# A hybrid Mamba-2 and block-attention trunk: x and the parameters handed over by channel, the weights in tiles

## Chip, cores and metric

The kernel runs on one core of a Trainium2 chip. The metric is the device time of one execution in microseconds (us). Most executions of one kernel agree within 0.3%.

## What is computed

Batch 1, 256 positions, 2048 channels, float32. One Mamba-2 layer, then keys and values from its output, one attention layer, and a last norm (all attention is within one block of 256 positions, so the reference's choice of blocks picks nothing):

```python
def reference(x, ...):
    h = rmsnorm(x, a_norm_g)                 # (1, 256, 2048)
    proj = h @ a_w_in                        # 2048 x 10304: z 4096, xBC 6144, dt 64
    xbc = silu(causal_depthwise_conv(proj[xBC], conv_w, conv_b))    # 4 taps: x 4096, B 1024, C 1024
    dt = softplus(proj[dt] + dt_bias); a = dt * -exp(A_log)
    y = ssd_chunked_scan(x * dt, a, B, C) + D * x                   # one chunk of 256
    y = grouped_rmsnorm(y * silu(z), gnorm_g, 8)
    x = x + y @ a_w_out                      # 4096 x 2048
    k, v = split(rmsnorm(x, kv_norm_g) @ w_kv); k = rope(k)         # 2048 x 4096
    q, z = split(rmsnorm(x, b_norm_g) @ b_w_in); q = rope(q)        # 2048 x 4096
    x = x + (causal_softmax_attention(q, k, v) * silu(z)) @ b_w_out # 16 heads of 128; 2048 x 2048
    return rmsnorm(x, final_norm_g)
```

## The kernel before

**The products.** Every large product is cut into blocks of 512 output columns, and a block into units of two k (a k is 128 channels of the contraction), so a unit has 256 x 512 weights, 512 KB. A unit goes through four steps: SP's queue loads it (`load`, tile `raw`, 4 buffers); ScalarE rounds it to the fast matmul format (`hi<-raw`); VectorE takes the rest (`lo<-raw,hi`; `hi` and `lo` have 5 buffers); TensorE multiplies it (`products`). The left operand is split in the same way into two halves (`hT` for the first layer, later `yn`, `kvop`, `bop`, `oop`), and a product of two split numbers is three matmuls of 128x512 each: high by high, low by high, high by low. There are two halves j of 128 positions, so a unit is 12 matmuls, and the sums `ps` of a block fill two banks of PSUM. Four banks are kept for such sums, the other four ("s") for transposes and small products.

**The order.** The program is written out in one order per engine. The list `ORDER` names the blocks of the first layer: `B0 d0 C0 x0 z0 ...` (B, C, x, z are columns of `a_w_in`; `d0` is the narrow dt block of 16 matmuls, one per k; `o` and `p` multiply by `a_w_out`). The main loop runs over the units `u`; it first emits the splits of units up to a look-ahead, each followed by the load of the unit four further on, and then the products of `u`. Between products, `some` emits pieces of side work (convolution, scan, norms, attention) when a model of the engines' clocks in the program says that their inputs are ready. So what is emitted early moves where later side work stands.

**The start.** `xl` holds x by position (two tiles of 128 positions, 2048 channels), loaded in four parts by `load_x`. For each of the 16 k, `h_gen` transposes both parts of x on TensorE (`s<-ident,xl`), and `operand` scales by the gain `g_a` and splits into `hT` (ScalarE the high half, VectorE the low). Three such k precede the first product, the other 13 stand between the products of block B0, whose units are u = 0 to 7. The gain itself comes as 16 rows (`ga`) and is transposed too. `squares` sums x squared along the channels, per position, in ScalarE and VectorE (`accum_out`). `first_norm` turns that into the factor `r` (`root`: a Sqrt on ScalarE and small VectorE steps). `parameters` transposes the other vectors on TensorE (`s<-ident,em`), which GpSimd's queue had loaded into `em`.

**After a block.** `turn` scales the finished bank by `r` (ScalarE `ps<-ps,r`), transposes 32x32 blocks on VectorE (`T<-ps`), writes to DRAM on SP's queue (`turned<-T`) and reads it back with GpSimd's queue (`U<-turned`, four transfers), which leaves the block by channel in `U`. `dt_evac` has TensorE transpose `r` right behind the dt block (`s<-ident,r`).

Of the kernel before, what the change touches and what calls it, by code (L numbers as in the profile page):

```python
# [173 lines left out]
def trunk_kernel(ctx: ExitStack, tc: tile.TileContext, x, a_norm_g, a_w_in, a_conv_w, a_conv_b,  # L174
                 a_dt_bias, a_A_log, a_D, a_gnorm_g, a_w_out, kv_norm_g, w_kv, b_norm_g, b_w_in,
# [134 lines left out]
    def load(u):  # L310
        if u >= len(units) or units[u][2] == 1:
            return
        b, k, _ = units[u]
        if b["form"] == "dt":
            t = wts.tile([P, 16, 64], F32, name="raw_dt", tag="raw")
            src = dram(b["w"], b["col"], [[b["ncols"], P], [P * b["ncols"], 16], [1, 64]])
# [37 lines left out]
    accs = {}  # L354
# [6 lines left out]
    def products(u):  # L361
        b, k, row = units[u]
        acc = accs.setdefault(id(b), {})
        if b["form"] == "dt":
            ps, w = bank("ps_dt"), HI.pop(u)
            for i in range(16):
                PE.matmul(ps, lhsT=w[:, i, :], rhs=b["operand"](i), start=i == 0, stop=i == 15)
            b["evac"](ps)
            some(4)
            return  # L370
        hi, lo, k0, k1 = HI.pop(u), LO.pop(u), b["ks"][0], b["ks"][-1]
        last = k + 1 == k1
        rows = (0, 1) if row is None else (row,)
        for j in rows:
            if k == k0:
                acc[j] = bank("ps")
            for i in range(2):
                xo = b["operand"](k + i)
                first, end = k + i == k0, k + i == k1
                xh, xl = xo[:, j * P:(j + 1) * P], xo[:, L + j * P:L + (j + 1) * P]  # L380
                PE.matmul(acc[j], lhsT=xh, rhs=hi[:, i, :], start=first, stop=False)
                PE.matmul(acc[j], lhsT=xl, rhs=hi[:, i, :], start=False, stop=False)
                PE.matmul(acc[j], lhsT=xh, rhs=lo[:, i, :], start=False, stop=end)
                if not end:
                    some(2)
            if last:
# [41 lines left out]
    ga = const.tile([16, P], F32, name="ga", tag="c1")  # L428
    SP.dma_start(ga, dram(a_norm_g, 0, [[P, 16], [1, P]]))
    xl = [big.tile([P, D], F32, name=f"xl{t}", tag=f"y{4 + t}") for t in range(2)]  # L430
    xv = x[0].rearrange("(t p) d -> p t d", p=P)

    def load_x(h):
        for t in range(2):
            SP.dma_start(xl[t][:, h * 512:(h + 1) * 512], xv[:, t, h * 512:(h + 1) * 512])  # L435

    load_x(0)
# [3 lines left out]
    em = take("em")  # L441
    vec = em[:112, 1, :P]
    row = 0
    for src, n in ((a_conv_b, 48), (a_gnorm_g, 32), (kv_norm_g, 16), (b_norm_g, 16)):
        POOL.dma_start(vec[row:row + n, :], dram(src, 0, [[P, n], [1, P]]))
        row += n
    cwr = em[:, 0, :256].rearrange("p (a b) -> p a b", a=2)[:96]
    POOL.dma_start(cwr, dram(a_conv_w, 0, [[P, 96], [96 * P, 2], [1, P]]))
    dta = const.tile([64, 2], F32, name="dta")
    POOL.dma_start(dta[:, 0:1], dram(a_dt_bias, 0, [[1, 64], [1, 1]]))  # L450
    POOL.dma_start(dta[:, 1:2], dram(a_A_log, 0, [[1, 64], [1, 1]]))
    dr = const.tile([32, 2], F32, name="dr")
    POOL.dma_start(dr, dram(a_D, 0, [[2, 32], [1, 2]]))
# [48 lines left out]
    early = big.tile([P, 2, 1024], F32, name="early", tag="y6")  # L502
# [9 lines left out]
    g_a = const.tile([P, 16], F32, name="g_a")  # L512
    pa = take("s")
    PE.transpose(pa[:, :16], ga, ident[:16, :16])
    ACT.activation(g_a, pa[:, :16], AF.Copy)
    banks.give((pa.tensor.name, pa.offset))
# [16 lines left out]
    gv = const.tile([P, 112], F32, name="gv")  # L533
    cbias = const.tile([P, 48], F32, name="cbias")
    g_gn, g_kv, g_b = gv[:, 48:80], gv[:, 80:96], gv[:, 96:112]
    dw = em[:32, 1, P:2 * P].rearrange("p (a b) -> p a b", a=2)
    Dv = const.tile([P, 32], F32, name="Dv")
    cw = const.tile([P, 192], F32, name="cw")
    negA = const.tile([64, 1], F32, name="negA")

    def parameters():

        p = take("s")
        PE.transpose(p[:, 0:32], dw.rearrange("p a b -> p (a b)"), ident[:32, :32])
        PE.transpose(p[:, 128:224], cwr[:, 0, :], ident[:96, :96])
        PE.transpose(p[:, 224:320], cwr[:, 1, :], ident[:96, :96])
        PE.transpose(p[:, 320:432], vec, ident[:112, :112])
        ACT.activation(Dv, p[:, 0:32], AF.Copy)
        ACT.activation(cw, p[:, 128:320], AF.Copy, scale=0.5)
        ACT.activation(gv, p[:, 320:432], AF.Copy)  # L550
        give(p, em)
        DVE.tensor_scalar(cbias, gv[:, 0:48], 0.5, None, op0=OP.mult)
# [19 lines left out]
    def h_gen():  # L572
        for k in range(16):
            p = take("s")[:, :L]
            for t in range(2):
# [3 lines left out]
            banks.give((p.tensor.name, p.offset))  # L579
# [389 lines left out]
    for name in ORDER:  # L969
        kind, i = name[0], int(name[1:])  # L970
        names[len(blocks)] = name
        if kind == "d":
            block(a_w_in, NIN, DI + CONV, range(16), h_op, "dt", dt_evac, "h")
        elif kind in "BCxz":
            col = {"B": 2 * DI, "C": 2 * DI + 1024, "x": DI, "z": 0}[kind] + 512 * i
            evac = {"B": lambda q: conv_evac(32 + 4 * q, ("B", q)), "C": c_evac, "x": x_evac, "z": z_evac}[kind](i)
            block(a_w_in, NIN, col, range(16), h_op, "x", evac, "h")
        else:
# [4 lines left out]
            block(a_w_out, D, 512 * n, ks, lambda k: yn[k // 4][:, k % 4, :], "x", out_evac(n, i < 10 and kind == "o", kind == "p"), "yn")  # L983
# [162 lines left out]
    for n in range(4):  # L1146
        block(w_kv, 2 * D, 512 * n, range(16), lambda k: B["kvop"][:, k, :], "x", k_evac(n), "kv")
    for n in range(4):
        block(w_kv, 2 * D, D + 512 * n, range(16), lambda k: B["kvop"][:, k, :], "x", v_evac(n), "kv")
    for kind, n in ("z0", "q0", "q1", "q2", "z1", "q3", "z2", "z3"):  # L1150
        n = int(n)
        if kind == "q":
            block(b_w_in, 2 * D, 512 * n, range(16), b_op, "x", q_evac(n), "b")
        else:
            block(b_w_in, 2 * D, D + 512 * n, range(16), b_op, "x", zb_evac(n), "b")
# [59 lines left out]
    for n in range(4):  # L1215
        block(b_w_out, D, 512 * n, range(16), lambda k: B["oop"][:, k, :], "rows" if n == 3 else "x",
# [7 lines left out]
    for h in range(1, 3):  # L1224
        load(2 * h - 2)
        load(2 * h - 1)
        load_x(h)
    part = split(0)
    for i in range(2):
        next(prep)  # L1230
        if not i:
            warm_up()
        part(i)
    next(prep)
    banks.give((warm.tensor.name, warm.offset))
    load(4)
    begun = 1
    for u in range(len(units)):
        while begun <= min(u + (1 if u < 7 else u - 5 if u < 7 + LOOK else LOOK), len(units) - 1):
            split(begun)()  # L1240
            load(begun + RAW_BUFS)
            if begun == 1:
                load_x(3)
            begun += 1
        if u in (1, 3, 5, 6):
            squares(u // 2)
        if u == 7:
            first_norm()
        if u == 2:
            DVE.tensor_copy(dw, dr[:, :, None].to_broadcast([32, 2, 64]))  # L1250
        if u == 7:
            parameters()
        b, k, _ = units[u]
# [12 lines left out]
_INS = ['x', 'a_norm_g', 'a_w_in', 'a_conv_w', 'a_conv_b', 'a_dt_bias', 'a_A_log', 'a_D', 'a_gnorm_g', 'a_w_out',  # L1266
        'kv_norm_g', 'w_kv', 'b_norm_g', 'b_w_in', 'b_w_out', 'final_norm_g']
# [13 lines left out]

# [21 lines left out]
```

## Time and profile before

| what | value |
|---|---|
| timed runs | 1135.43, 1135.71 (median), 1139.35 us |
| span of the profiled execution | 1140.6 us |
| TensorE busy | 1123.2 us (98%), 5153 matmuls |
| VectorE, ScalarE, GpSimd busy | 852.6, 643.9, 145.1 us |
| DMA | 267.29 MB, 234 GB/s mean |
| granted TensorE clock, mean | 0.996 |

The span runs from the first to the last instruction or landing of one execution taken by the profiler; the page gives no other time for that execution. It lies 4.9 us above the median of the timed runs and 1.2 us above the slowest. Line 130 in the rows is the wrapper through which every instruction of TensorE, VectorE and ScalarE is recorded, so rows are told apart by their tiles. In a row of a timeline stand the start and duration in us, the engine, the operation, `output<-inputs`, the shapes and a count; in square brackets the idle time before it and what ended it.

### The profile page before, as it was taken

What the parts mean: (1) busy time and instruction counts of PE and PEld (TensorE: products, weight loads), DVE (VectorE), ACT (ScalarE), POOL (GpSimd) and SP (SyncE); (2) the same over time, 40 slices, a digit from 0 to 9 for tenths busy, and PEclk for the clock granted to TensorE, in tenths of its full rate; (3) what the DMA queues carried; (4) which work ended last, traced back from release to release, by engine and by line L of the source; (5) the groups of instructions that cost most, each with busy time, mean ns of one, the idle gap of its engine ahead of it and who ended that gap; (6) DMA issues with size and microseconds to landing.
All of it is one profiled execution on the core that took longest, in us unless ns stands there. A gap on an engine that the chain in (4) does not pass through costs nothing.

```text
span 1140.6 us, 14865 instructions
## 1 busy us (share of the span) xinstructions
PE 1123.2 (98%) x5153; PEld 918.7 (81%) x5153; DVE 852.6 (75%) x1316; ACT 643.9 (56%) x896; POOL 145.1 (13%) x255
## 2 busy tenths in 40 slices
PE   9999999999999999999999999999999999999996
PEld 6887888888787888888888888878888888888885
DVE  5786968877868969697987667877445687797564
ACT  5566757765857757567654574434443444444453
POOL 2011121121011021112111000000000011222000
PEclk9999999999999999999999999999999999999999
DMA  8778999897887888888887557768757777989752
GB/s 264 221 230 236 272 251 288 243 284 219 243 246 223 255 242 264 253 237 252 263 253 238 194 178 222 203 200 245 238 172 243 214 224 241 269 247 260 254 202 92
DMA packets 133403, 267.29 MB, mean 234 GB/s; under 512 B 13712, under 2 KB 14560, under 8 KB 133200
## 3 DMA queue, kind: packets, MB, share of 16 engines
q1 hardware_dynamic: 120384, 230.20, 64.9%
q0 software_dynamic: 12944, 36.15, 13.4%
q8 instruction: 40, 0.66, 0.2%
q14 instruction: 35, 0.29, 0.1%
HBM read 240.03 MB, written 26.28 MB: 233 GB/s over the span
## 4 chain that ended last, share of the span: by engine, by line
PE 81%; DVE 7%; DMA 6%; issue 3%; ACT 2%; POOL 0%; SPq 0%; DVEq 0%; ACTq 0%; POOLq 0%
PE ps L130 76%; PE s L130 5%; DMA U<-turned 2%; DVE lo L130 2%; DVE xs L130 2%; DMA raw<-in_a_w_in_dram 1%; DVE T L130 1%; DMA raw<-in_w_kv_dram 1%; ACT hi L130 1%; DMA turned<-T 1%; DVE K L130 1%; POOL U L415 0%; ACT xs L130 0%; ACT u L130 0%; SPq L435 0%
## 5 line engine op out<-in xcount | busy, mean ns | idle before, releaser
L130 DVE TENSOR_TENSOR lo<-raw,hi 128x1024 fp32r<-128x1024 f32 (+1 forms) x385 | 463.5, 1215 | 172.6 <-ACT hi L130 171.6
L130 ACT ACTIVATE hi<-raw 128x1024 fp32r<-128x1024 f32 (+1 forms) x385 | 397.3, 1051 | 261.4 <-PE ps L130 120.1
L130 PE MATMUL ps<-hi,hT 128*128 128x512 f32 x1280 | 399.7, 393 | 0.2 <-DVE hT L130 0.2
L130 PEld LDWEIGHTS ps<-hi,hT 128*128 128x128 f32 x1280 | 238.1, 188 | 49.0 <-issue 0.7
L130 PE MATMUL ps<-lo,hT 128*128 128x512 f32 x640 | 250.5, 391 | 0.0
L130 PE MATMUL ps<-hi,bop 128*128 128x512 f32 x512 | 160.7, 395 | 0.0
L130 PE MATMUL ps<-hi,yn 128*128 128x512 f32 x512 | 159.5, 393 | 0.0
L130 PE MATMUL ps<-hi,kvop 128*128 128x512 f32 x512 | 158.4, 390 | 0.0
L415 POOL DMA_DIRECT2D U<-turned x128 | 74.2, 586 | 654.3 <-DMA turned<-T 293.0
L130 PEld LDWEIGHTS ps<-lo,hT 128*128 128x128 f32 x640 | 120.6, 188 | 27.2 <-DVE lo L130 2.0
L130 PEld LDWEIGHTS ps<-hi,bop 128*128 128x128 f32 x512 | 95.8, 188 | 19.5
L130 PEld LDWEIGHTS ps<-hi,kvop 128*128 128x128 f32 x512 | 95.6, 188 | 19.6
L130 PEld LDWEIGHTS ps<-hi,yn 128*128 128x128 f32 x512 | 94.8, 188 | 19.7 <-issue 0.7
L130 PE MATMUL ps<-lo,kvop 128*128 128x512 f32 x256 | 100.0, 390 | 2.2 <-DVE lo L130 2.2
L130 PE MATMUL ps<-lo,yn 128*128 128x512 f32 x256 | 100.1, 391 | 0.7 <-DVE lo L130 0.7
L130 PE MATMUL ps<-lo,bop 128*128 128x512 f32 x256 | 99.7, 389 | 0.0
L130 PE MATMUL ps<-hi,oop 128*128 128x512 f32 x256 | 79.6, 392 | 0.0
L130 DVE SCALAR_TENSOR_TENSOR xs<-u,cw,xs 128x255 f32<-128x255 f32 (+2 forms) x144 | 59.3, 476 | 0.0
L130 PEld LDWEIGHTS ps<-lo,kvop 128*128 128x128 f32 x256 | 48.0, 188 | 13.0 <-DVE lo L130 3.1
L130 PEld LDWEIGHTS ps<-lo,yn 128*128 128x128 f32 x256 | 48.1, 188 | 11.6 <-DVE lo L130 1.5
L130 PEld LDWEIGHTS ps<-lo,bop 128*128 128x128 f32 x256 | 48.1, 188 | 10.3
L130 PEld LDWEIGHTS ps<-hi,oop 128*128 128x128 f32 x256 | 47.9, 188 | 9.8
(172 smaller groups left out, 944.9 us busy)
## 6 DMA issues: line engine op xcount, KB each, us to landing
raw<-in_a_w_in_dram SPq DMA_DIRECT2D x159, 512.0 KB, 5.3
raw<-in_a_w_out_dram SPq DMA_DIRECT2D x64, 512.0 KB, 5.5
raw<-in_w_kv_dram SPq DMA_DIRECT2D x64, 512.0 KB, 4.7
raw<-in_b_w_in_dram SPq DMA_DIRECT2D x64, 512.0 KB, 5.0
turned<-T SPq DMA_DIRECT2D x64, 256.0 KB, 4.6
U<-turned POOLq DMA_DIRECT2D x128, 128.0 KB, 6.8
raw<-in_b_w_out_dram SPq DMA_DIRECT2D x32, 512.0 KB, 5.5
em<-AC POOLq DMA_DIRECT2D x32, 256.0 KB, 7.4
```

What stands on the lines that cost most here:

```text
L130: return call(out, *args, **kw)
L415: POOL.dma_start(U[32 * q:32 * q + 32].rearrange("p (b c) -> p b c", b=8), src)
```

## The change

The host hands over x a second time by channel (`xT`, 128 x 16 x 256), all per-channel vectors as one array of 128 rows (`params`), the two per-head vectors as `heads`, and every weight matrix as tiles of 256 x 512, in which one of the 128 partitions has its two rows side by side (4 KB where it was 2 KB twice).

- x is loaded by channel into `xt` (nine loads, two of 1 k and seven of 2 k); `hT` is made from it with no transpose. The 32 transposes of x, the one of the gain and the four of the parameters are gone.
- The parameters come with two loads on SP's queue behind the split of unit 3; the gain `g_a` comes with a load on ScalarE's own queue. GpSimd's eight loads at the start are gone. The halving of two vectors is moved to VectorE, at u = 9.
- The squares of x are now summed by channel: ScalarE squares 512 columns (2 k), VectorE adds them to a running sum, eight times. The sum over the 128 channels of a partition block is four matmuls by a column of ones (`s<-ones,early`), in the middle of the dt block, behind its sixth matmul.
- The norm's factor therefore comes later: `first_norm` stands in the dt block, and the two results of B0 are held until then (`held`). Before, `first_norm` stood ahead of B0's last unit and the results left at its end.
- The look-ahead at u = 7, 8, 9 is 1, 2, 3 units where it was 2, 3, 4.

```diff
-        if u in (1, 3, 5, 6):
-            squares(u // 2)
+        if 1 <= u <= 7:
+            squares(u - 1)
         if u == 7:
-            first_norm()
-        if u == 2:
-            DVE.tensor_copy(dw, dr[:, :, None].to_broadcast([32, 2, 64]))
-        if u == 7:
+            squares(7)
             parameters()
...
     def squares(h):
-        ACT.activation(early[:, 0, :512], xl[0][:, h * 512:(h + 1) * 512], AF.Square, accum_out=ss[:, 0, h:h + 1])
-        v = xl[1][:, h * 512:(h + 1) * 512]
-        DVE.scalar_tensor_tensor(early[:, 1, :512], v, 1.0, v, op0=OP.mult, op1=OP.mult, accum_out=ss[:, 1, h:h + 1])
+        total, s = early[:, 0, :512], early[:, 1, h % 2 * 512:(h % 2 + 1) * 512]
+        v = xt[h // 4][:, h % 4 * 2:h % 4 * 2 + 2, :].rearrange("p k l -> p (k l)")
+        ACT.activation(s if h else total, v, AF.Square)
+        if h:
+            DVE.tensor_add(total, total, s)
...
     def first_norm():
-        DVE.tensor_reduce(nt[:, 0, :], ss, axis=mybir.AxisListType.X, op=OP.add)
+        p = take("s")
+        for t in range(2):
+            for i in range(2):
+                PE.matmul(p[:, t:t + 1], lhsT=early[:, 0, i * L + t * P:i * L + (t + 1) * P], rhs=ones[:, 0:1],
+                          start=i == 0, stop=i == 1)
+        DVE.tensor_copy(nt[:, 0, :], p[:, 0:2])
         root(nt, D)
...
             for i in range(16):
+                if i == 6:
+                    first_norm()
+                    for acc, j in held:
+                        blocks[0]["evac"](acc, j)
                 PE.matmul(ps, lhsT=w[:, i, :], rhs=b["operand"](i), start=i == 0, stop=i == 15)
...
     def h_gen():
         for k in range(16):
-            p = take("s")[:, :L]
-            for t in range(2):
-                PE.transpose(p[:, t * P:(t + 1) * P], xl[t][:, k * P:(k + 1) * P], ident)
-            operand(hT[:, k, :], p, g_a[:, k:k + 1])
+            operand(hT[:, k, :], xt[k // 8][:, k % 8, :], g_a[:, k:k + 1])
...
-            t = wts.tile([P, 2, 512], F32, name="raw", tag="raw")
-            src = dram(b["w"], k * P * b["ncols"] + b["col"], [[b["ncols"], P], [P * b["ncols"], 2], [1, 512]])
...
+            t = RAW[0] if half else wts.tile([P, 2, 512], F32, name="raw", tag="raw")
+            if half is None:
+                SP.dma_start(t.rearrange("p i c -> p (i c)"), b["w"][b["n"], k // 2])
```

Three places show what moves. First, TensorE's own list from the start of the program: `early` is a tile of ones for warm-up matmuls. Before:

```order
L130 MATMUL s<-ident,xl_76 128x128
L130 MATMUL s<-ident,xl_77 128x128
L130 MATMUL ps<-hi,hT 128x512 x2
L130 MATMUL ps<-lo,hT 128x512
L130 MATMUL ps<-hi,hT 128x512 x2
L130 MATMUL ps<-lo,hT 128x512
```

and at the dt block and what follows it:

```order
L130 MATMUL ps_dt<-hT,dtp 128x512 x16
L130 MATMUL s<-ident,r_113 128x128 x2
L130 MATMUL ps<-hi,hT 128x512 x2
L130 MATMUL ps<-lo,hT 128x512
L130 MATMUL ps<-hi,hT 128x512 x2
```

After, the same place at the dt block:

```order
L130 MATMUL ps_dt<-hT,dtp 128x512 x6
L130 MATMUL s<-ones,early 128x1 x4
L130 MATMUL ps_dt<-hT,dtp 128x512 x10
L130 MATMUL s<-ident,r_99 128x128 x2
L130 MATMUL ps<-hi,hT 128x512 x2
```

The pair of transposes that stood in front of every sixth product of B0 is gone, and four matmuls of one column stand in the dt block.

Second, ScalarE around the first norm, from the split of the dt weights (`dtp`) to the results of B0. Before:

```order
L130 ACTIVATE dtp<-raw_dt 128x16x64
L130 ACTIVATE hi<-raw 128x1024
L130 ACTIVATE r_113<-r_113 128x2
L130 ACTIVATE Dv<-s 128x32
L130 ACTIVATE cw<-s 128x192
L130 ACTIVATE gv<-s 128x112
L130 ACT_TABLE_LOAD
L130 ACTIVATE negA<-dta 64x1
L130 ACTIVATE ps<-ps,r_113 128x512 x2
```

After:

```order
L130 ACTIVATE dtp<-raw_dt 128x16x64
L130 ACTIVATE early<-xt_77 128x512 x2
L130 ACT_TABLE_LOAD
L130 ACTIVATE negA<-dta 64x1
L130 ACTIVATE hi<-raw 128x1024 x2
L130 ACT_TABLE_LOAD
L130 ACTIVATE r_99<-r_99 128x2
L130 ACTIVATE ps<-ps,r_99 128x512 x2
L130 ACTIVATE dtw<-ps_dt 64x256
```

The Exp for `negA` now stands ahead of the Sqrt for `r`, so the Sqrt needs its table again, and a third load follows later for the next Exp; two splits stand ahead of the Sqrt.

Third, VectorE where the second convolution of C ends (`xs<-u,xs`), to which TensorE's product of C with B (`s<-xs`) comes later. Before:

```order
L130 TENSOR_TENSOR lo<-raw,hi 128x1024
L130 SCALAR_TENSOR_TENSOR xs<-u,cw,xs 128x255 x4
L130 SCALAR_TENSOR_TENSOR xs<-u,cw,xs 128x254 x4
L130 TENSOR_TENSOR lo<-raw,hi 128x1024
L130 SCALAR_TENSOR_TENSOR xs<-xs,Dv,s 128x256 x2
L130 SCALAR_TENSOR_TENSOR xs<-u,cw,xs 128x253 x4
L130 TENSOR_TENSOR lo<-raw,hi 128x1024
L130 SCALAR_TENSOR_TENSOR xs<-xs,Dv,s 128x256 x2
L130 TENSOR_TENSOR lo<-raw,hi 128x1024
L130 SCALAR_TENSOR_TENSOR xs<-u,xs 128x1024
```

After:

```order
L130 TENSOR_TENSOR lo<-raw,hi 128x1024
L130 TENSOR_TENSOR xs<-xs,z_1873 128x512
L130 SCALAR_TENSOR_TENSOR xs<-u,par,xs 128x254 x4
L130 TENSOR_TENSOR lo<-raw,hi 128x1024 x2
L130 TENSOR_TENSOR squares<-squares 128x512
L130 TENSOR_TENSOR squares<-squares 128x256
L130 SCALAR_TENSOR_TENSOR xs<-u,par,xs 128x253 x4
L130 TENSOR_TENSOR lo<-raw,hi 128x1024 x2
L130 SCALAR_TENSOR_TENSOR xs<-u,xs 128x1024
```

The convolution's last four steps lie over more `lo`. Counted from the first product, TensorE's first product of this C with B stands behind 1444 main products instead of 1426, and VectorE's step that it needs stands behind one `lo` more. For the first C the numbers are 382 instead of 379, behind as many `lo` as before. Other side work of the first layer moves by up to 108 products either way; from the attention layer on, the orders are the same but for a few neighbours.

More of the change, by code (lines that the diff above doesn't have):

```diff
@@ L282, in trunk_kernel, with block @@
     blocks = []
-    def block(w, ncols, col, ks, operand, form, evac, key):
-        blocks.append(dict(w=w, ncols=ncols, col=col, ks=ks, operand=operand, form=form, evac=evac, key=key))
+    def block(w, n, ks, operand, form, evac, key):
+        blocks.append(dict(w=w, n=n, ks=ks, operand=operand, form=form, evac=evac, key=key))
     units = []
@@ L308, in trunk_kernel, with load @@
     loads, copies, ended = [0.0], [0.0], {}
-    def load(u):
+    def load(u, half=None):
         if u >= len(units) or units[u][2] == 1:
@@ L385, in products @@
                     some(2)
-            if last:
+            if last and u == 7:
+                held.append((acc[j], j))
+            elif last:
                 b["evac"](acc[j], j)
@@ L425, in in_32s, with load_x @@
         return a.rearrange("p j (b l) -> p j b l", l=32)
-    ga = const.tile([16, P], F32, name="ga", tag="c1")
-    SP.dma_start(ga, dram(a_norm_g, 0, [[P, 16], [1, P]]))
-    xl = [big.tile([P, D], F32, name=f"xl{t}", tag=f"y{4 + t}") for t in range(2)]
+    g_a = const.tile([P, 16], F32, name="g_a")
+    nc.scalar.dma_start(g_a, params[:, :16])
+    xt = [big.tile([P, 8, L], F32, name=f"xt{t}", tag=f"y{4 + t}") for t in range(2)]
     xv = x[0].rearrange("(t p) d -> p t d", p=P)
-    def load_x(h):
-        for t in range(2):
-            SP.dma_start(xl[t][:, h * 512:(h + 1) * 512], xv[:, t, h * 512:(h + 1) * 512])
-    load_x(0)
+    def load_x(k, n):
+        SP.dma_start(xt[k // 8][:, k % 8:k % 8 + n, :], xT[:, k:k + n, :])
+    load_x(0, 1)
     ident = const.tile([P, P], F32, name="ident")
     make_identity(nc, ident)
[L441 to L448, printed above, removed]
+    par = const.tile([P, 336], F32, name="par")
     dta = const.tile([64, 2], F32, name="dta")
[L450 to L453, printed above, removed]
     tri = const.tile([P, 384], F32, name="tri", tag="c0")
@@ L511, in trunk_kernel @@
     warm_up()
[L512 to L516, printed above, removed]
     warm_up()
@@ L522, in squares @@
     def squares(h):
-        ACT.activation(early[:, 0, :512], xl[0][:, h * 512:(h + 1) * 512], AF.Square, accum_out=ss[:, 0, h:h + 1])
-        v = xl[1][:, h * 512:(h + 1) * 512]
-        DVE.scalar_tensor_tensor(early[:, 1, :512], v, 1.0, v, op0=OP.mult, op1=OP.mult, accum_out=ss[:, 1, h:h + 1])
-    def first_norm():
-        DVE.tensor_reduce(nt[:, 0, :], ss, axis=mybir.AxisListType.X, op=OP.add)
+        total, s = early[:, 0, :512], early[:, 1, h % 2 * 512:(h % 2 + 1) * 512]
[3 more added lines that the diff above has]
+            DVE.tensor_add(total, total, s)
+    def first_norm():
+        p = take("s")
[4 more added lines that the diff above has]
+        DVE.tensor_copy(nt[:, 0, :], p[:, 0:2])
+        give(p)
         root(nt, D)
         DVE.tensor_scalar(r0h, r0, 0.5, None, op0=OP.mult)
[L533 to L538, printed above, removed]
+    cbias, cw = par[:, 0:48], par[:, 112:304]
+    g_gn, g_kv, g_b, Dv = par[:, 48:80], par[:, 80:96], par[:, 96:112], par[:, 304:336]
     negA = const.tile([64, 1], F32, name="negA")
     def parameters():
[L543 to L552, printed above, removed]
         ACT.activation(negA, dta[:, 1:2], AF.Exp)
@@ L1215, in trunk_kernel @@
     for n in range(4):
-        block(b_w_out, D, 512 * n, range(16), lambda k: B["oop"][:, k, :], "rows" if n == 3 else "x",
+        block(b_w_out, n, range(16), lambda k: B["oop"][:, k, :], "rows" if n == 3 else "x",
               last_evac if n == 3 else fin_evac(n), "op")
@@ L1223, in trunk_kernel @@
     prep = h_gen()
[L1224 to L1227, printed above, removed]
+    load(0, 0)
+    load_x(1, 1)
+    load(0, 1)
+    for h in range(1, 4):
+        load_x(2 * h, 2)
+        load(h)
     part = split(0)
@@ L1238, in trunk_kernel @@
     for u in range(len(units)):
[L1239 removed]
+        while begun <= min(u + (1 if u < 8 else 2 if u < 9 else LOOK), len(units) - 1):
             split(begun)()
             load(begun + RAW_BUFS)
[L1242 to L1243 removed]
+            if begun < 4:
+                load_x(8 + 2 * begun, 2)
+            if begun == 3:
+                SP.dma_start(par, params[:, 16:])
+                SP.dma_start(dta, heads)
             begun += 1
[L1245 to L1246 removed]
+        if 1 <= u <= 7:
+            squares(u - 1)
         if u == 7:
[L1248 to L1251 removed]
+            squares(7)
             parameters()
+        if u == 9:
+            DVE.tensor_scalar(par[:, 0:48], par[:, 0:48], 0.5, None, op0=OP.mult)
+            DVE.tensor_scalar(cw, cw, 0.5, None, op0=OP.mult)
         b, k, _ = units[u]
@@ L1279, in _rope_table, with _laid_out, tiles, channels @@
                                  dtype=f)
+def _laid_out(inputs):
+    import numpy as _np
+    def tiles(w):
+        k, n = w.shape
+        return w.reshape(k // 256, 2, 128, n // 512, 512).transpose(3, 0, 2, 1, 4).reshape(n // 512, k // 256, 128, 1024)
+    def channels(v):
+        return v.reshape(-1, 128).T
+    i = {n: _np.asarray(a) for n, a in inputs.items()}
+    w = i["a_w_in"][0]
+    first = w.shape[1] - 64
+    dt = w[:, first:].reshape(16, 128, 64).transpose(1, 0, 2).reshape(128, 1024)
+    conv = _np.concatenate([channels(i["a_conv_w"][0][t]) for t in range(4)], axis=1)
+    d = _np.repeat(i["a_D"][0].reshape(32, 2), 64, axis=1).T
+    params = _np.concatenate([channels(i["a_norm_g"]), channels(i["a_conv_b"]), channels(i["a_gnorm_g"]),
+                              channels(i["kv_norm_g"]), channels(i["b_norm_g"]), conv, d], axis=1)
+    heads = _np.stack([i["a_dt_bias"][0], i["a_A_log"][0]], axis=1)
+    xt = i["x"][0].T.reshape(16, 128, 256).transpose(1, 0, 2)
+    return [("x", i["x"]), ("xT", xt), ("params", params), ("heads", heads), ("a_w_in", tiles(w[:, :first])), ("a_w_dt", dt),
+            ("a_w_out", tiles(i["a_w_out"][0])), ("w_kv", tiles(i["w_kv"])), ("b_w_in", tiles(i["b_w_in"][0])),
+            ("b_w_out", tiles(i["b_w_out"][0])), ("final_norm_g", i["final_norm_g"]), ("rope_cs", _rope_table())]
 def kernel(**inputs):
@@ L1290 @@
     arrays, args = {}, []
[L1291 removed]
+    named = [(n, _np.ascontiguousarray(a)) for n, a in _laid_out(inputs)]
     for name, a in named:
```

41 lines of the change are left out of this document (15 added, 26 removed).

## The prediction

> **What bounds the kernel now.** I read the page first, then the stretches of the span, then what TensorE waits for, and last the start instruction by instruction.
>
> ```profile
> span 1140.6 us, 14865 instructions
> PE 1123.2 (98%) x5153; PEld 918.7 (81%) x5153; DVE 852.6 (75%) x1316; ACT 643.9 (56%) x896; POOL 145.1 (13%) x255
> ```
>
> TensorE is busy 98% of the span; no other engine comes near. Time can only come out of TensorE's own work, its idle time, or the two ends.
>
> ```profile
> core 0: us, PE busy (x) PEld busy (x) DVE busy (x) ACT busy (x) POOL busy (x), PEclk, DMA share, GB/s
> 7.80:14.80 7.00, 7.00 (x32) 4.90 (x31) 4.92 (x8) 5.04 (x10) 0.00 (x0) 1.00 1.01 358
> 14.80:34.70 19.90, 19.66 (x97) 15.47 (x96) 15.52 (x28) 13.21 (x24) 0.00 (x0) 1.00 0.73 225
> 34.70:38.50 3.80, 3.80 (x19) 3.09 (x19) 2.21 (x12) 2.74 (x8) 0.00 (x0) 1.00 0.74 240
> 38.50:1131.80 1093.30, 1086.81 (x4999) 893.02 (x4997) 825.66 (x1256) 618.50 (x847) 139.08 (x238) 1.00 0.79 235
> ```
>
> The stretches are: the first product to the end of unit 1, the rest of B0, the dt block, and all the rest up to the last product. In the last one TensorE idles only 1093.3 - 1086.8 = 6.5 us. What it waits for there:
>
> ```profile
> PE s L130 <- DVE xs L130: 3.5, 2, 2.3
> PE ps L130 <- DVE lo L130: 2.9, 3, 1.8
> 356.80:359.10 2.30, 0.04 (x2) 0.03 (x1) 2.30 (x3) 2.30 (x4) 0.00 (x0) 1.00 0.97 342
> 360.40:363.90 3.50, 3.50 (x10) 2.72 (x9) 3.47 (x6) 2.58 (x5) 0.00 (x0) 0.51 0.91 295
> ```
>
> Five waits, all for VectorE, sum to 6.4 us. Behind the longest, 2.3 us at 356.8, the granted clock is 0.51 for 3.5 us, which costs another 3.5 x 0.49 = 1.7 us. So 8.2 us hang on waits in the body, and the change cannot touch more there.
>
> **The transposes of x.** These rows give the price of a pair in B0, and of six products with none between.
>
> ```profile
> 18.55 0.38 PE L130 MATMUL s<-ident,xl 128*128 128x128 f32 x2
> 20.14 0.38 PE L130 MATMUL s<-ident,xl 128*128 128x128 f32 x2
> 39.28 0.62 PE L130 MATMUL ps<-hi,hT 128*128 128x512 f32 x2
> 40.64 0.62 PE L130 MATMUL ps<-hi,hT 128*128 128x512 f32 x2
> 31.48 0.66 PE L130 MATMUL s<-ident,em 32*128 32x32 f32 x4
> 31.90 0.71 PE L130 MATMUL ps<-hi,hT 128*128 128x512 f32 x2
> ```
>
> With a pair, six products take 20.14 - 18.55 = 1.59 us; without, 40.64 - 39.28 = 1.36 us, 0.227 each. A pair costs 0.23 us and the four transposes of the parameters 0.42 us, all on the path, since TensorE has no idle time there. From 14.8 us on B0 holds six units, 72 products: 72 x 0.227 = 16.3 us where the stretch took 19.9. That is 3.6 us less: ten or eleven pairs (2.4), the parameters (0.4), and the rest small gaps.
>
> This holds if VectorE keeps up. In the new B0 it has per unit one `lo`, two `hT` and one add of 512 columns. The nearest rows, by their starts:
>
> ```profile
> 10.70 1.23 DVE L130 TENSOR_TENSOR lo<-raw,hi 128x1024 fp32r<-128x1024 f32 x1 [0.81 <-ACT hi L130]
> 11.84 0.48 DVE L130 SCALAR_TENSOR_TENSOR hT<-s,g_a,hT 128x256 fp32r<-128x256 f32 x1
> 15.22 0.69 DVE L130 SCALAR_TENSOR_TENSOR early<-xl 128x512 f32<-128x512 f32 x1
> 15.83 0.87 DVE L130 SCALAR_TENSOR_TENSOR hT<-s,g_a,hT 128x256 fp32r<-128x256 f32 x2
> 16.68 1.22 DVE L130 TENSOR_TENSOR lo<-raw,hi 128x1024 fp32r<-128x1024 f32 x1
> ```
>
> `lo` 11.84 - 10.70 = 1.14, the add like the square 15.83 - 15.22 = 0.61, two `hT` 16.68 - 15.83 = 0.85: 2.60 us against TensorE's 2.72. It fits with 5% to spare. If the overlaps between instructions were lost (1.22 + 0.87 + 0.69 = 2.78), VectorE would set the pace and cost 6 x 0.06 = 0.4 us.
>
> **The first two units.** No transpose stands ahead of the first product, so it can start earlier than 7.8. But unit 1 waits for its weights:
>
> ```profile
> 9.61 1.06 ACT L130 ACTIVATE hi<-raw 128x1024 fp32r<-128x1024 f32 x1 [0.47 <-DMA raw<-in_a_w_in_dram]
> 14.58 0.39 PE L130 MATMUL ps<-lo,hT 128*128 128x512 f32 x1
> ```
>
> Counted on SP's queue, 1544 KB had been ordered up to and with unit 1's weights; after the change it is 1536 KB. So they land at 9.6 again. The new order then makes VectorE finish `lo` of unit 1 (11.84, as in its row) before the low half of `hT` for k = 2 (12.3); eleven products from there end at 12.3 + 2.5 = 14.8, where unit 1 ended before (14.58 + 0.23). I take a gain of 0 here; the bounds are 0.5 us either way, from a landing earlier (GpSimd's eight small loads no longer share the engines) or later (1 KB rows in the first two loads of x). B0 then ends at 14.8 + 16.3 = 31.1 instead of 34.7.
>
> **The four products by ones** are new in the dt block; the trace has no matmul of one column. Bounds from both sides:
>
> ```profile
> 34.74 3.79 PE L130 MATMUL ps_dt<-hT,dtp 128*128 128x512 f32 x16
> 38.37 0.38 PE L130 MATMUL s<-ident,r 128*128 128x128 f32 x2
> 38.50 0.71 PE L130 MATMUL ps<-hi,hT 128*128 128x512 f32 x2
> 101.01 0.92 PE L130 MATMUL s<-xs 128*128 128x256 f32 x4 [1.23 <-DVE xs L130]
> 101.69 0.71 PE L130 MATMUL ps<-hi,hT 128*128 128x512 f32 x2
> ```
>
> At the cheap end they cost what two transposes cost in front of a product (38.50 - 38.37 = 0.13), so 0.27 for four. At the dear end, like the two float32 products at 101.01, each shown as two matmuls: 0.68 us, 0.34 each, so 1.4 for four. A gain is excluded, since nothing is removed there. They are float32 products, so they are nearest to the dear row, but stream one column instead of 256 or 128: I take 0.9. The dt block took 38.37 - 34.74 = 3.63; C0's first product then starts at 31.1 + 3.63 + 0.9 + 0.13 = 35.8, against 38.5: **2.7 us earlier**.
>
> **The norm's chain, now inside the dt block.** TensorE needs `r` right behind the dt block (`s<-ident,r`), and B0's first bank six products later.
>
> ```profile
> 35.34 0.15 DVE L130 TENSOR_REDUCE r<-ss 128x2 f32<-128x8 f32 x1
> 36.76 0.16 DVE L130 TENSOR_TENSOR r<-r 128x2 f32<-128x2 f32 x1
> 36.41 1.28 ACT L130 ACT_TABLE_LOAD   x1
> 37.70 0.20 ACT L130 ACTIVATE negA<-dta 64x1 f32<-64x1 f32 x1
> 37.81 1.20 ACT L130 ACTIVATE ps<-ps,r 128x512 f32<-128x512 f32 x2
> 38.48 1.31 DVE L130 STREAM_TRANSPOSE T<-ps 128x512 f32<-128x512 f32 x2 [0.39 <-ACT ps L130]
> ```
>
> The sums are there at 31.1 + 6 x 0.227 + 0.9 = 33.4; from the first step to `r` it took 36.92 - 35.34 = 1.58, so 35.0; TensorE asks for it at 35.6. Scaling and transposing the first bank took 38.48 + 0.66 - 37.81 = 1.3, so the bank is free at 36.3; TensorE wants it at 35.8 + 1.36 = 37.1. Both hold, with 0.6 and 0.8 us to spare, so I price the move at 0. The load of the Sqrt table (1.29 from 36.41 to 37.70) stands behind two splits and needs no operand, so it runs while VectorE makes `lo` of the last one (1.14). If it fell into the chain whole, TensorE would wait 1.29 - 0.6 = 0.7 us. What is queued behind the late Sqrt is the scaling, the dt copy and the splits of C0's third and later units; two units (5.4 us) are split ahead of it. The Trainium skill (page "ScalarE: Activation LUTs", section "What ACT_TABLE_LOAD costs") adds a drain of about 1380 ns to each switch of table. By it, a load that fell into the chain whole would be an estimated 2.7 instead of 1.29, and C0 would start 2 us later instead of 0.7. The trace does not agree: `negA` starts 1.29 us after the load's start.
>
> **Loads.** GpSimd's eight loads, the copy into `em`, three small copies and the accumulator reads go; all lay beside TensorE's work, and cost nothing now. The weights' rows:
>
> ```profile
> q1 hardware_dynamic: 120384, 230.20, 64.9%
> q0 software_dynamic: 12944, 36.15, 13.4%
> raw<-in_a_w_in_dram SPq DMA_DIRECT2D x159, 512.0 KB, 5.3
> U<-turned POOLq DMA_DIRECT2D x128, 128.0 KB, 6.8
> ```
>
> Half as many packets may land a little sooner, but in the body no wait of TensorE ends with a weight load, so by itself this is 0 to a few tenths.
>
> **The body's waits.** Side work moves, so the waits are drawn anew. At the longest, TensorE asks 18 products later (4.1 us), VectorE answers one `lo` and its share of side work later (2.7 us): 1.4 of 2.3 us go, and the drop of the clock (1.7) may go with them. At the first C, TensorE asks 3 products later: 0.7 of 1.2 go. That could be 2 to 4 us; but some twenty other pieces moved, and each may open a wait. Bounds: all 8.2 us go, or as many come. I count 1.
>
> **The sum** against the profiled execution: 1140.6 - 2.7 - 1.0 = 1136.9. The median is 4.9 us under that span, perhaps because its waits are not all in every run; I carry the difference, -3.7, over to the median: 1135.7 - 3.7 = **1132.0 us**. The bound between a change and none is 0.5% (5.7 us), about what a measurement of this kernel tells apart.
>
> **Rivals.**
> 1. The start pays as worked out and the body's waits close as well. For it: all five end with VectorE, whose work before the second C is spread over more units. Against it: twenty other moves. It takes over half of the 8.2 us: 1135.7 - 2.7 - 5 = 1128, down to 1125 if all go.
> 2. The gain is given back at the norm's chain: sums dear (1.4 instead of 0.9), VectorE's pace (0.4), and the chain waiting for the table (0.7). The margins of 0.6 and 0.8 us are small, which speaks for it; that the splits' weights had landed by then without a wait speaks against it. 1135.7 - 2.7 + 0.5 + 0.4 + 0.7 = 1134.6, and about 1137 if a late split adds to the wait and the clock drops behind it as at 360.4.
> 3. Slower: larger packets of weights hold up `U`. By the rows, a packet of q1 takes 0.649 x 16 x 1140.6 / 120384 us = 98 ns for 1912 B, one of q0 189 ns for 2793 B; at q1's rate it would be 143, so it loses 46 ns beside the other queue. If that doubles with the weights' packets, each of four transfers (47 packets on 16 engines) loses 0.14 us, so `U` comes 0.55 us later. There are 32 turns; TensorE loses more than 0.5% on the whole from (5.7 + 3.7) / 0.55 = 17 turns on, at 1141.4 or more. Against it: TensorE's waits now are five, and `U` has slack in most. With three to eight turns on the path it is 1134 to 1136, no change. The Trainium skill's "DMA: Bandwidth & Descriptors" (section "Queues, rings and completion order") says that an engine goes round its queues packet by packet, which is this rival's mechanism; no row here shows the turns themselves.
>
> **Chances.** The forecast 0.53 (its own range 1129.5 to 1134.5); rival 1 0.24; rival 2 and the mild form of rival 3 0.16; slower 0.07. The range leaves out about 1 in 10 at each end: 1126 to 1138. Faster by over 0.5% (under 1130.0): rival 1 and a little of the forecast, 0.28; slower (over 1141.4) 0.07; between them 0.65.
>
> **What would show it.** C0's first product at 35.8 (34.6 to 37.3) instead of 38.5; B0 at 16.3 us from unit 2 on with no gap; two `r` transposes right behind the dt block; the four products by ones 0.3 to 1.4 us; no idle time of TensorE over 2 us near the second C, and a clock that stays at 1.00 there. The forecast is wrong if TensorE idles behind the dt block, if VectorE is full through B0, or if the body's idle time moves by more than 3 us from 6.5.

## The result, and the profile after

Six runs of the changed kernel took 1128.14 to 1130.84 us, median 1129.97; the kernel before, on the same chip, took 1135.43 to 1142.76, median 1136.56. Two runs far off all others of their kernel, 1248.66 us of the kernel before here and 1414.93 us of one version below ("Another order"), were disturbed and are left out. The ratio is 0.993, with a 95% interval of 0.9911 to 0.9948: 0.7% faster, or 8 us by the ratio (5.9 to 10.1) and 6.6 by the medians, since before scatters upwards. The profiled execution took 1128.18 us, of which its span is 1126.5, so a span is 1.7 us shorter than the time. By that difference the profiled execution of before, with its span of 1140.6, took an estimated 1142.3 us, as long as the slowest of its timed runs.

The page of the changed kernel, its head and queues:

```profile
span 1126.5 us, 14807 instructions
PE 1114.4 (99%) x5122; PEld 915.7 (81%) x5122; DVE 854.2 (76%) x1315; ACT 648.5 (58%) x894; POOL 142.1 (13%) x247
...
q1 hardware_dynamic: 69776, 230.37, 62.2%
q0 software_dynamic: 12672, 35.99, 12.0%
...
raw<-in_a_w_in_dram SPq DMA_DIRECT2D x159, 512.0 KB, 4.7
...
U<-turned POOLq DMA_DIRECT2D x128, 128.0 KB, 5.8
```

The same bytes go in 69776 packets where it was 120384. The weights land in 4.7 us where it was 5.3, and `U`, on the other queue, in 5.8 where it was 6.8. What TensorE waits for in the changed kernel, and its stretches (the first product to the end of unit 1, the rest of B0, and from C0 to the last product):

```profile
PE s L130 <- DVE early L130: 1.2, 1, 1.2
PE ps L130 <- ACT hi L130: 1.1, 1, 1.1
PE ps L130 <- DVE hT L130: 0.8, 1, 0.8
PE ps L130 <- ACT hT L130: 0.4, 1, 0.4
4.00:14.80 10.80, 8.39 (x28) 4.94 (x27) 6.30 (x10) 7.16 (x13) 0.00 (x0) 1.00 0.96 348
14.80:30.60 15.80, 15.80 (x72) 13.07 (x71) 15.60 (x25) 15.62 (x27) 0.00 (x0) 1.00 0.86 281
35.52:1117.96 1082.44, 1082.44 (x4999) 892.39 (x4996) 825.33 (x1256) 619.87 (x847) 140.47 (x238) 1.00 0.75 237
```

All four waits lie ahead of 12 us. In the last stretch busy time and length are equal: the five waits of the body are gone. With the same count of products that stretch is 1082.4 us long where it was 1093.3. Of these 10.9 us, 6.5 were idle time and 1.7 the slowed clock; most of the other 2.7 lie at the same five places, as the first experiment shows. Since the profiled execution of before was a long one, the difference of the spans, 14.1 us, is more than that of the timed runs, and its 6.5 us of waits are more than an execution of median length can have lost.

The start, in TensorE's timeline (the row of the ones has eight records for its four float32 products):

```profile
5.05 1.14 PE L130 MATMUL ps<-hi,hT 128*128 128x512 f32 x2
...
10.59 0.50 PE L130 MATMUL ps<-hi,hT 128*128 128x512 f32 x1 [0.43 <-ACT hT L130]
11.85 0.50 PE L130 MATMUL ps<-hi,hT 128*128 128x512 f32 x1 [0.77 <-DVE hT L130]
...
30.80 1.52 PE L130 MATMUL ps_dt<-hT,dtp 128*128 128x512 f32 x6
32.16 0.95 PE L130 MATMUL s<-ones,early 128*128 128x1 f32 x8
32.96 2.58 PE L130 MATMUL ps_dt<-hT,dtp 128*128 128x512 f32 x10
35.38 0.38 PE L130 MATMUL s<-ident,r 128*128 128x128 f32 x2
35.52 0.71 PE L130 MATMUL ps<-hi,hT 128*128 128x512 f32 x2
```

The dt block begins at 30.80, the ones take 32.96 - 32.16 = 0.80 us, and C0's first product starts at 35.52 where it was 38.50. The norm's chain beside it, VectorE's and ScalarE's timeline of the changed kernel:

```profile
33.14 0.16 DVE L130 COPY r<-s 128x2 f32<-128x2 f32 x1 [0.65 <-PE s L130]
...
34.56 0.16 DVE L130 TENSOR_TENSOR r<-r 128x2 f32<-128x2 f32 x1
30.95 1.28 ACT L130 ACT_TABLE_LOAD   x1
33.54 0.20 ACT L130 ACTIVATE r<-r 128x2 f32<-128x2 f32 x1 [1.31 <-DVE r L130]
34.82 1.24 ACT L130 ACTIVATE ps<-ps,r 128x512 f32<-128x512 f32 x2 [1.08 <-DVE r L130]
```

`r` is ready at 34.72 and asked for at 35.38. The table's load ends at 32.23, and ScalarE then waits 1.31 us for VectorE: the load is hidden.

### The profile page after: what moved, and what is told of

Same layout as the page of the kernel before. It is cut to its first block, busy times and chain, and to the rows that moved or that the text cites. A ratio compares the mean times of both kernels' runs of the same rounds, so it can differ in the third digit from the quotient of the medians.

```text
span 1126.5 us, 14807 instructions
## 1 busy us (share of the span) xinstructions
PE 1114.4 (99%) x5122; PEld 915.7 (81%) x5122; DVE 854.2 (76%) x1315; ACT 648.5 (58%) x894; POOL 142.1 (13%) x247
## 3 DMA queue, kind: packets, MB, share of 16 engines
q1 hardware_dynamic: 69776, 230.37, 62.2%
## 4 chain that ended last, share of the span: by engine, by line
PE 98%; DMA 1%; DVE 0%; SPq 0%; issue 0%; ACT 0%; DVEq 0%; ACTq 0%
PE ps L130 93%; PE s L130 5%; DMA raw<-in_a_w_in_dram 1%; PE ps_dt L130 0%; DVE x L130 0%; SPq L437 0%; ACT hi L130 0%; DVE sfin L130 0%; SPq L321 0%; DVE hT L130 0%; DVE T L130 0%; DVEq L1301 0%; ACT sfin L130 0%; DVE lo L130 0%; ACTq L130 0%
## 5 line engine op out<-in xcount | busy, mean ns | idle before, releaser
L130 DVE SCALAR_TENSOR_TENSOR xs<-u,par,xs 128x255 f32<-128x255 f32 (+2 forms) x144 | 59.8, 477 | 0.4 <-ACT xs L130 0.4
L130 DVE STREAM_TRANSPOSE T<-ps 128x512 f32<-128x512 f32 x64 | 43.9, 703 | 17.7 <-ACT ps L130 11.5
L130 ACT ACTIVATE em<-em,dal 128x128 f32<-128x128 f32 (+1 forms) x128 | 54.4, 448 | 3.8 <-DMA em<-AC 1.8
L130 PEld LDWEIGHTS ps<-lo,yn 128*128 128x128 f32 x256 | 48.1, 188 | 10.1
```

What stands on the lines that cost most here:

```text
L130: return call(out, *args, **kw)
```

## Experiments

Three theories were to be told apart for what the body's waits were worth. A: they went because the start moved the side work, and the form of the weights is worth nothing. B: they went because weights in tiles land sooner. C is the prediction's third rival: larger packets hold up `U`, so that tiles cost time, and the rest of the change pays for it. The kernel before had medians of 1136.83 us (29 runs, beside the first four below) and 1135.75 (17 runs, beside the other four). Versions of different groups are best compared by their ratios to it.

**The tiles alone.** The kernel before, its order of instructions kept, with the weights handed over in tiles:

```diff
-            src = dram(b["w"], k * P * b["ncols"] + b["col"], [[b["ncols"], P], [P * b["ncols"], 2], [1, 512]])
+            w = b["w"][b["col"] // 512, k // 2]
...
-            SP.dma_start(t, src)
+                SP.dma_start(t.rearrange("p i c -> p (i c)"), w)
```

> The kernel before with only its weights laid out in tiles (4 KB packets); every engine's order stays as before. Theory A (the body's waits closed because the side work stands in another order): TensorE still waits some 4 to 6 us in the body, at the same places (near 99, 285, 357, 765, 791 us); the time is 0 to 1.5 us under before. Theory B (they closed because the tiles land sooner, 4.7 us after issue instead of 5.3): the waits fall under 2 us in all and the time is 4 to 6 us under before, ratio near 0.996. Theory C (the packets hold up U): U lands later than 6.8 us after issue and the time rises.

1132.19 us (12 runs), ratio 0.9963 (0.9947 to 0.998). B is right here and C falls: 4 to 5 us from the tiles with no other change (2 to 6 by the interval). From its page and TensorE's waits:

```profile
q1 hardware_dynamic: 69440, 230.20, 62.7%
q0 software_dynamic: 12944, 36.15, 13.7%
raw<-in_a_w_in_dram SPq DMA_DIRECT2D x159, 512.0 KB, 5.0
U<-turned POOLq DMA_DIRECT2D x128, 128.0 KB, 6.3
PE ps L130 <- DVE hT L130: 0.2, 1, 0.2
PE ps L130 <- ACT hi L130: 0.2, 1, 0.2
38.45:1121.00 1082.55, 1082.55 (x4999) 892.06 (x4996) 825.62 (x1255) 618.94 (x847) 139.08 (x238) 1.00 0.77 237
```

The start is as before (C0 at 38.45), but the body has no wait left. Both kernels have the same order of instructions, so their profiles can be set side by side product by product. From C0 to the last product the kernel before takes 10.5 us longer, and 9.7 of these arise at the five waits: 1.5 around 101 us, 1.2 at 286, 4.2 at 359, 2.1 at 767 and 0.8 at 792.

How a faster load took away waits for VectorE is seen by going back from the longest of them, TensorE's 2.26 us ahead of 359.10. Rows of ScalarE, VectorE and TensorE in the kernel before:

```profile
331.23 1.06 ACT L130 ACTIVATE hi<-raw 128x1024 fp32r<-128x1024 f32 x1 [2.11 <-DVE nt L130]
339.24 1.06 ACT L130 ACTIVATE hi<-raw 128x1024 fp32r<-128x1024 f32 x1 [6.95 <-DMA raw<-in_a_w_out_dram]
340.33 1.23 DVE L130 TENSOR_TENSOR lo<-raw,hi 128x1024 fp32r<-128x1024 f32 x1 [3.57 <-ACT hi L130]
357.73 1.22 DVE L130 SCALAR_TENSOR_TENSOR xs<-u,xs 128x1024 f32<-128x1024 f32 x1
359.10 0.89 PE L130 MATMUL s<-xs 128*128 128x256 f32 x4 [2.26 <-DVE xs L130]
```

ScalarE's split waits 6.95 us for a load, and VectorE's `lo` 3.57 us for that split. The same two splits, the same `lo` and the same `xs` with tiles, from ScalarE's and VectorE's timelines:

```profile
329.42 1.06 ACT L130 ACTIVATE hi<-raw 128x1024 fp32r<-128x1024 f32 x1 [2.88 <-DMA raw<-in_a_w_out_dram]
333.10 1.06 ACT L130 ACTIVATE hi<-raw 128x1024 fp32r<-128x1024 f32 x1 [2.62 <-DVE xd L130]
334.19 1.22 DVE L130 TENSOR_TENSOR lo<-raw,hi 128x1024 fp32r<-128x1024 f32 x1 [1.11 <-ACT hi L130]
351.59 1.22 DVE L130 SCALAR_TENSOR_TENSOR xs<-u,xs 128x1024 f32<-128x1024 f32 x1
```

The splits are 3.7 us apart where they were 8.0. VectorE's `lo` starts 6.14 us earlier (334.19 against 340.33), and so does `xs` (351.59 against 357.73): in the 17.4 us between them VectorE makes up nothing of the delay. TensorE itself was only 3.6 us later there than with tiles, and so it waited. The sixteen DMA engines are full around there. The DMA view of 318 to 342 us of the kernel before, then of 316 to 336 with tiles (tenths of engine time in 40 slices, and the loads' median time to landing in that stretch):

```profile
DMA  4899977999999999999999999999999999995200
...
raw<-in_a_w_out_dram SPq DMA_DIRECT2D x4, 512.0 KB, 11.7
```

```profile
DMA  7899894488999999999998999999999899999521
...
raw<-in_a_w_out_dram SPq DMA_DIRECT2D x4, 512.0 KB, 10.3
```

So these loads, four in each stretch, land 1.4 us sooner where the engines are full.

**The change without tiles.** The changed kernel, its order of instructions kept, with the weights in rows as before:

```diff
-                SP.dma_start(t.rearrange("p i c -> p (i c)"), b["w"][b["n"], k // 2])
+                SP.dma_start(t, dram(b["w"], k * P * ncols + col, [[ncols, P], [P * ncols, 2], [1, 512]]))
```

> The changed kernel with its weights in rows as before (two packets of 2 KB per partition), all else and every engine's order as changed. Theory A: about 1130 us, at most 1 us over the changed kernel, body's waits under 1.5 us. Theory B: weight loads land 5.3 us after issue again, body's waits of 4 to 6 us come back, time near 1135 us. The start: C0's first product within 0.5 us of 35.5 by both.

1132.2 us (1129.98 to 1136.54, 12 runs), ratio 0.9963 (0.9945 to 0.9981). This lies between A and B. C0 starts at 35.96. Two of TensorE's rows:

```profile
PE ps L130 <- ACT hi L130: 1.9, 2, 1.6
...
PE ps L130 <- DVE lo L130: 0.5, 1, 0.5
```

The longest wait in them, 1.57 us, lies at 7.74, in the start. In the body TensorE waits 1.2 us in all (0.35 and 0.5 of these rows, and two waits of 0.2), so the waits are as A had them, while the time, 2.2 us above the changed kernel, is not. From C0 to the last product this execution takes 1085.1 us where the changed kernel took 1082.4; the difference arises near these waits, around 287, 306 and 329 us.

The rest of the change is thus worth 4 to 5 us without tiles, and the tiles 2 to 4 us on top (2.2 by the two medians, 3.7 by the two ratios, with an interval of about 2 us either way). Either part alone removes most of the body's waits, so their gains overlap.

**The transposes put back.** The changed kernel with 14 pairs of transposes in B0 that nothing reads:

```diff
-                next(prep, None)
+                if next(prep, 0) is None:
+                    for t in range(2):
+                        nc.tensor.transpose(idle[:, t * P:(t + 1) * P], xt[0][:, 0, t * P:(t + 1) * P], ident)
```

> The changed kernel with 14 pairs of 128x128 transposes put back between the products of B0, at the places where they stood; their results are read by nobody. All else as changed. By the prediction's price of 0.23 us a pair C0's first product starts 3.2 us later (38.7 instead of 35.5), and the time rises by as much, to about 1133 us, since nothing in the body can take it up. Rival: the body has slack for a late start, and the time rises by less than 1 us.

1132.94 us (12 runs), ratio 0.9963 (0.9947 to 0.998): 3.0 us above the changed kernel by the medians, 3.7 by the ratios, where 3.2 was expected. Two pairs in TensorE's timeline, with six products between their starts:

```profile
18.33 0.38 PE L394 MATMUL s<-ident,xt 128*128 128x128 f32 x2
19.93 0.38 PE L394 MATMUL s<-ident,xt 128*128 128x128 f32 x2
```

They are 1.60 us apart, as before the change (1.59). The time of the transposes is what the prediction took it for. C0's start, though, missed what was expected: 40.56 in the profiled execution, not 38.7. There TensorE waited 0.82 and 0.76 us for `hT`, at 11.0 and 12.3, and its granted clock was then 0.50 from 13.3 to 16.7. This execution (1133.65 us) is one of the longer ones.

**Another order.** The kernel before, in which the model that places the side work counts x's transposes as taking no time. Nothing is computed differently; only the order of emission is drawn anew:

```diff
+            at = PE.ns
             for t in range(2):
                 PE.transpose(p[:, t * P:(t + 1) * P], xl[t][:, k * P:(k + 1) * P], ident)
+            PE.ns = at
```

> The kernel before with the same instructions and data, but the model of the engines' clocks that places the side work counts the transposes of x as taking no time; so the side work of the first layer stands elsewhere (some 180 rows of TensorE's list differ). Theory A: the body's waits are drawn anew, between 1 and 8 us in other places, and the time moves by 1 to 5 us either way. Theory B: the waits stay near 6 us in all and the time within 1.5 us of before.

1158.41 us (five runs), ratio 1.0193 (1.0159 to 1.0228): 22 us slower, many times what was expected. TensorE now waits for `yn`, the left operand of the first layer's products with `a_w_out`:

```profile
PE ps L130 <- ACT yn L130: 13.2, 3, 7.1
```

The two longest of these waits are 7.14 us at 551 and 5.31 us at 648.

**Packets or places.** The kernel before with tiles that lie together in DRAM, 512 KB each, but with the two rows of a partition apart, so that its reads are still 2 KB:

```diff
-            src = dram(b["w"], k * P * b["ncols"] + b["col"], [[b["ncols"], P], [P * b["ncols"], 2], [1, 512]])
+            w = b["w"][b["col"] // 512, k // 2]
...
-            SP.dma_start(t, src)
+                SP.dma_start(t, w.rearrange("i p c -> p i c"))
```

> The kernel before with its weights in tiles of 512 KB that lie together in DRAM, but each partition's two rows apart from each other, so that the packets stay 2 KB (about 120,000 on SP's queue instead of 69,000); every engine's order as before. If the packets' size gave the 4.6 us of the kernel with plain tiles, this one is back at 1136 to 1137 us with waits of 4 to 6 us in the body. If it was that a load reads one stretch of DRAM instead of 256 rows far apart, it stays at 1132 us, with waits under 1 us.

1137.35 us (12 runs), ratio 1.0012 (0.9999 to 1.0025): nothing is gained, where whole tiles gave 0.9963. So at 2 KB a packet it is worth nothing that the tile lies together in DRAM; the gain needs the larger packets. The time came as expected, the waits did not: the body of the profiled execution (1136.18 us) has 3.0 us of them instead of 4 to 6, and 1.4 of these are for a load in the attention layer. ScalarE's waits for all weight loads sum to 134.5 us in this profile and to 122.1 in that of before, against 109.8 with whole tiles; in the changed kernel they are 91.8, and 126.9 with its weights in rows. From the page:

```profile
q1 hardware_dynamic: 118464, 230.20, 64.6%
```

In engine time for all of q1 (share x 16 x span) it is 11,840 us before, 11,730 here, and 11,330 with whole tiles: a packet takes 98 ns for 1912 B before and 163 ns for 3315 B, so 4% less for a byte.

**`hT` first.** The changed kernel, with the low and high halves for k = 2 and 3 made ahead of unit 1's split; TensorE's order stays:

```diff
     load(4)
+    next(prep)
+    next(prep)
```

> The changed kernel with the two operands of unit 1 (hT for k = 2 and 3) made ahead of that unit's weight split, on ScalarE and VectorE; TensorE's order is the same. Read from the changed kernel's rows: VectorE ends lo of unit 1 at 11.3 us and hT after it at 11.7, and TensorE waits to 11.85; with hT first, lo ends at 11.3 and TensorE needs it for its third product, so unit 1 ends 0.7 us earlier. Time 0.7 us under the changed kernel (1129.3), or 2 us under it in the runs in which the start's gaps no longer drop the clock for 3.4 us. Rival: the weights' landing sets both, and nothing changes.

1128.13 us (1127.78 to 1130.78, 6 runs), ratio 0.9926 (0.991 to 0.9942). This is the lowest median of all, 1.8 us under the changed kernel. But by the ratios (0.9926 against 0.993) the two differ by only 0.5 us, and their intervals overlap, so a gain is not shown. In the profiled execution C0 starts at 35.51, as in the changed kernel (35.52). The waits for `hT` are gone from TensorE's list. Of two short ones for `lo` one stands in their place, at 12.1, and the other lies in the body, at 754:

```profile
PE ps L130 <- DVE lo L130: 0.7, 2, 0.4
```

**Another order of the changed kernel.** 100 ns are added to the model's TensorE clock at u = 9:

```diff
         if u == 9:
+            PE.ns += 100.0
```

> The changed kernel with the same instructions and data, but the model's clock of TensorE set 100 ns ahead once, at unit 9, so that the side work of the first layer stands in another order (some 170 rows of TensorE's list differ). If the order of the side work is a matter of luck that the changed kernel happened to have, the time moves up by 1 to 20 us, with waits of TensorE in the body that the changed kernel does not have. If tiles close the waits whatever the order, it stays within 1.5 us of 1130.

1148.39 us (4 runs), ratio 1.0102 (1.0085 to 1.012): 18 us above the changed kernel by the medians, 20 by the ratios, although every instruction is the same but for its place. TensorE's waits for `yn`, and two stretches at half clock, of which the first began within the longest wait and the other right behind the second longest (the last three figures of a stretch are clock, DMA share and GB/s):

```profile
PE ps L130 <- ACT yn L130: 10.9, 3, 5.6
539.62:546.45 6.83, 3.67 (x8) 2.58 (x9) 6.83 (x13) 5.08 (x10) 0.00 (x0) 0.50 0.58 193
638.61:645.43 6.82, 6.35 (x14) 4.69 (x15) 2.34 (x2) 1.73 (x2) 0.00 (x0) 0.50 0.24 77
```

The body has 13.4 us of waits, 12.6 of them for the two halves of `yn`. In the two slow stretches TensorE is busy 3.67 + 6.35 = 10.0 us at half clock, an estimated loss of 5.0 more; together that is about the 18 us. The two longest waits, at 542 and 639, are those at which the other order lost its time as well.

**A later norm.** The changed kernel with the sums and the norm behind the twelfth product of the dt block instead of the sixth:

```diff
-                if i == 6:
+                if i == 12:
```

> The changed kernel with the first norm behind the twelfth matmul of the dt block instead of the sixth; the body's side work falls into another order too, so only the stretch to C0 is read. By the changed kernel's rows (sums asked for at 32.2, r ready 2.6 us later) r is ready at 36.1 while TensorE asks at 35.4: a wait of 0.7 us in front of s<-ident,r and C0 at 36.2 instead of 35.5. If the chain had more slack than the 0.7 us in the rows, C0 stays at 35.5; if the table load falls into it, the wait is 1.3 us longer.

1147.48 us (2 runs), ratio 1.0093 (1.0069 to 1.0117). The time tells nothing on the norm, since this edit too drew the body's order anew (11.3 us of waits for `yn`). The start does: TensorE waits for `r` behind the dt block, by the 0.7 us that were expected, and C0's first product starts at 36.55 (36.2 was expected):

```profile
36.39 0.40 PE L130 MATMUL s<-ident,r 128*128 128x128 f32 x2 [0.72 <-DVE r L130]
```

## Why the prediction was right or wrong

The time came inside the range, 2 us under the figure, and just inside the forecast's own range (from 1129.5), but the mechanism is that of the first rival: the start as worked out, and the body's waits gone. The figure looks better than it was. The kernel before was 0.85 us slower in these runs than in those that the forecast started from, so the gain is 6.6 us by the medians, or 8 by the ratio, where 3.7 was forecast. The likeliest class, no change, was wrong, by the median narrowly (1129.97 against the bound of 1130.0). Of the prediction's own signs of being wrong, one came in full, the body's idle time going from 6.5 us to 0, and one almost: VectorE was nearly full through B0.

- **The start** was right: B0 from unit 2 on (16.33 us against 16.3), the ones (0.80 against 0.9) and C0 (35.52 against 35.8) came as summed, and 3.0 us were gained where 2.7 were forecast. VectorE, busy 15.60 of 15.80 us, was nearly full through the rest of B0, yet TensorE did not wait there. The first two units ended 0.3 us earlier than the 14.8 worked out, inside the bounds: products began at 5.05 and then waited three times for splits, and the last wait was for the low half of `hT`, as forecast, but ended at 11.85 instead of 12.3, since ScalarE could split unit 1 at 9.08 instead of 9.6.
- **The norm's chain** at 0 was right, and its margin was 0.66 us against the 0.6 worked out; the later norm used it up, with a wait of 0.72. The Sqrt table's load took 1.28 us and was hidden.
- **The step that failed is the one on loads**: "in the body no wait of TensorE ends with a weight load, so by itself this is 0 to a few tenths". The rows were read rightly, and the conclusion did not follow. TensorE's waits named VectorE, VectorE had waited for ScalarE, and ScalarE for a load. At the longest wait a load's delay passed through both engines and reached TensorE 20 us later. The tiles, priced at nearly nothing, were worth 4 to 5 us in the order of before, and 2 to 4 in the new one; with the same tiles in packets of 2 KB nothing was gained.
- **The body's waits** by the moved side work were counted at 1 us, with bounds of 8.2 either way. Without tiles the change gave 4.6 us by the medians; less 2.5 (C0 at 35.96) to 3.0 for the start, that is 1.6 to 2.1 us, with an interval of about 2 us either way. The term may have been somewhat small. The 8.2 us that it was taken from belonged to a long execution: with tiles alone, which left no wait in the body, 4.6 us were gained by the medians. The waits near the second C went, as the reasoning had it; but they also went with tiles in the order of before, so that reasoning alone is not shown to be their cause.
- **Larger packets hold up `U`** is refuted. A packet of q0 takes 189 ns before and 191 with tiles (0.137 x 16 x 1129.7 / 12944), where the rival had 46 ns more, and `U` landed 0.5 us sooner.
- **The bound on a new order** was far too narrow. "As many come" put 8.2 us on it; the redrawn order of before lost 22 us, and the two of the changed kernel lost 18 and, with the later norm, 17.5. The prediction had reasons for the places near the two Cs only; that the change drew a good order in all others, with `yn` in time, was luck.

Split by the medians, the gain is 2.5 to 3.0 us for the start, 1.6 to 2.1 for the body's order and 2.2 for the tiles: 6.8, where the two kernels timed side by side were 6.6 apart by medians and 8 by the ratio. Each of the last two parts is uncertain by about 2 us.

What stays open: why a byte takes 4% less engine time in the larger packets, and which of the model's choices makes the products with `a_w_out` wait for `yn`.

## What to carry to other kernels

An engine named as the releaser of a wait may itself have been late: follow it back until an engine that waited for a transfer, and look at that engine's own list of waits for loads before pricing a faster load at nothing. Where the transfer engines are full in a stretch, a layout that gives each partition one row of 4 KB instead of two of 2 KB can pay, even if the loads seem hidden on the whole. Waits read from one profile are those of that execution: compare its span with the timed runs before pricing them. Where a model of clocks draws the order, every edit draws it anew, and 100 ns in it moved this kernel by 18 us: try an edit with its order held fixed, and its order without the edit.

## What was not expected of the hardware

Two short waits can be followed by a while at a lower clock. In the version with `hT` first (windows of the start; after the five engines' busy times come the granted clock, the DMA share and the rate), TensorE waited 0.60 and 0.48 us between 4.0 and 7.7, and the clock was then 0.52 for 3.5 us:

```profile
4.00:7.70 3.70, 2.62 (x7) 0.78 (x5) 2.23 (x5) 2.57 (x6) 0.00 (x0) 1.00 0.80 282
7.70:11.20 3.50, 3.50 (x9) 2.48 (x9) 1.22 (x4) 1.68 (x4) 0.00 (x0) 0.52 0.99 368
```

With the transposes put back the same happened later, 0.54 from 13.0 to 16.6, and in the changed kernel without tiles it was 0.50 from 8.5 to 11.9, behind one wait of 1.57. Such a stretch costs up to 3.5 x 0.48 = 1.7 us. With `hT` first it cost less than that against the changed kernel, since TensorE worked slowly through the time in which the changed kernel waited, and C0 started as early. The profiled execution of the changed kernel idled 2.3 us in its start and had no slow stretch. The Trainium skill ("TensorE: Matmul & The Clock Gate", section "HAM oscillation — how this bites in real kernels") puts the limit at idle gaps of about 3.4 us. The length of the slow stretch in these starts, 3.4 us, agrees with that figure. The gaps do not: 2.26 us near the second C of the kernel before were enough, 1.57 without tiles, and here 0.60 and 0.48. Longer gaps had longer slow stretches: with the waits of 5.0 to 7.1 us for `yn` in the three redrawn orders the clock was 0.50 for 6.8 to 10.2 us.
